# One fixed order for prompt attention and the sample tokens' cached attention

## The chip, the cores and the metric

The kernel runs on one core of a Trainium2 chip. The metric is device time in microseconds (us) of one execution, the median of three runs. The core has five engines with queues of their own: TensorE (PE, matrix products and transposes), VectorE (DVE), ScalarE (ACT), GpSimd (POOL) and SyncE (SP, which issues most transfers). PE writes only into PSUM, eight banks of 128 partitions x 512 floats; DVE and ACT copy from there.

## What is computed

One step of a one-layer decoder, for a prompt of 1024 tokens and for 8 sample tokens at position 4096: a half step of a SwiGLU network (1024 to 2816 features and back), a token mixer, a second half step, with norms before each. The mixer has four GLA heads (a recurrence with gates) and four MLA heads (attention over a compressed latent). The change lies in the mixer. Its two attentions are, in short:

```
# prompt, per head and block of 128 queries
s = (q_nope @ k_nope.T + q_pe @ k_pe.T) * scale      # keys up to the query
o = softmax(s) @ v                                    # k_nope = lat @ w_uk, v = lat @ w_uv
# sample tokens, 4096 cached keys and the token's own, absorbed form
s = (q_lat @ lat_all.T + q_pe @ pe_all.T) * scale     # q_lat = q_nope @ w_uk.T
o = (softmax(s) @ lat_all) @ w_uv
y = concat([y_gla, y_mla]) @ w_out
```

The cached latents lie in pages, and a page table says where.

## The kernel before, in words

Every large product is made from fp32 operands split in a high and a low part (`split`, L84 to L86: ACT writes the high part, DVE the difference), and `mm3` (L88 to L95) adds three passes: high x high, high x low, low x high.

A tile framework builds the program. Each tile comes from a pool with a number of buffers for its tag; a new tile waits until an old one of its tag has been read for the last time, and a pool that is opened where another was closed waits for that one's tiles. A planner at build time sets the order of each engine's instructions by the place in the text, earlier first, with what is ready; `tc.high_priority` moves some ahead. At run time each engine runs its queue in that order.

The stages that matter here, in the order of the text: the GLA of the prompt, in `levels` and `chunks(0)` to `chunks(3)` (L990 to L1025, two chunks of 128 tokens each, each needing the state that the one before left); between them `gate(0)` to `gate(3)` (L1071 to L1078), each 72 matmuls over the mixer's input; `gate_out` writes the gated outputs to DRAM (`ygs`). Before, `gate(3)` stands after `chunks(3)`.

Then comes the attention of the sample tokens. It is cut in 16 units, two groups of four tokens times eight stretches of 512 keys. `dec_unit` (L1157) fetches four latent tiles `kvt` and four rotary tiles `pet` with eight indirect transfers that POOL issues (L908), turns them with PE transposes against an identity into the bank `pd` (L1168, L1176; 24 transposes, copied out as `peT` by DVE and `latT` by ACT), makes the scores (L1181, L1184), the softmax (L1154, L1155), turns the probabilities (L1190) and multiplies them with the latents (L1195). `dec_combine` adds the token's own key and joins the eight parts. Two units are made before the prompt's attention (`decode(2)`), then one after each of its sixteen steps.

A step of the prompt's attention is a head h (four) and a block m of 256 queries (four). `scores(m)` projects the queries, makes for both blocks of 128 queries up to two score tiles `sc` (L1355 to L1361), takes the maximum on DVE (L1363), the exponentials on ACT (L1370) and scales them on DVE (L1376). `outputs` of the step before then turns the probabilities (L1391, m + 1 groups of four transposes), splits them (`pT_h`, `pT_l`) and multiplies with the values into `po`. For each pair of heads the rotary queries are made first (`rope`, L789 to L800), then the values; for each head the keys.

After the attention the GLA outputs come back (`yraw`, L1432 to L1437; POOL's small copy from `ym_h` holds the load back) and are split to `yg_h`, `yg_l`, and `project` (L1445) multiplies with `w_out`. `raw` is a tag with four buffers of 4 KB.

Of the kernel before, what the change touches and what calls it, by code (L numbers as in the profile page):

```python
# [10 lines left out]
F32 = mybir.dt.float32  # L11
# [30 lines left out]
def host_constants():  # L42
    """Tables that follow from the shapes alone."""
# [25 lines left out]
def hybrid_step(ctx: ExitStack, tc: tile.TileContext, I, O, C):  # L69
# [44 lines left out]
    # ------------------------------------------------------------------ norm statistics  # L114
# [7 lines left out]
    def sumsq(acc, sqp, src, m, n, eng=None):  # L122
        """acc[:, :n] (+)= src^2 for feature tile m."""
# [7 lines left out]
    def token_rstd(r, acc, sqp, L, inv_n):  # L131
        """r[:, i] = 1/sqrt(mean + eps) of the i-th 128 of L tokens, from the per-partition partial sums acc."""
# [10 lines left out]
    def spread_all(R, r, sqp, L, scale=1.0):  # L143
        """R[:, token] = scale * r on every partition, for L tokens."""
# [8 lines left out]
    def rstd(R, acc, sqp, s, inv_n, scale=1.0):  # L153
        """R = scale / sqrt(mean + eps) of block s on every partition."""
# [5 lines left out]
    def spread(r, sqp, ps, n, scale=1.0):  # L160
        """ps = scale * r, one value per token on its partition, on every partition."""
# [62 lines left out]
    def left_blocks(w, p, plain=False):  # L224
        """For the outputs 2p and 2p + 1 (of 128 features each) of w."""
# [56 lines left out]
    def eight(A, B, n, evict, between=None):  # L282
        """The plain products: evict(o, C[o // 2][o % 2])."""
# [9 lines left out]
    def first_steps(wg, wu, B, k0, loaded, between=None):  # L293
        """The first k0 pairs of outputs for the first tokens, from plain products."""
# [12 lines left out]
    # The down product is cut in the same way, with the even and the odd tiles of hidden features as the halves of features in.  # L307
    # Its right-hand blocks, in the order t1, t2, t3, t4, B11, B21, B22; two tiles of features of both chunks at a time.
# [5 lines left out]
    def sums_out(c, p, b, t):  # L314
        """Right-hand blocks of the hidden features 2p and 2p + 1, b = B11, B12, B21, B22; t is scratch."""
# [9 lines left out]
    def gate_up(wg, wu, B, k0, start, loaded):  # L325
        """silu(wg x) * (wu x) in hd; the first k0 pairs of outputs are made for the second tokens only, at the end."""
# [19 lines left out]
    def quarter(Q, pl, wd, name, order):  # L346
        """Name aij: the half j of the features in (even or odd tiles) to the half i of the features out."""
# [101 lines left out]
    # ================================================================== load x, first half step  # L449
# [15 lines left out]
    def token_factor(i, c):  # L465
        """1 / rms of 128 tokens, one on each partition: for the first tokens on a diagonal, for the others times x in place."""
# [23 lines left out]
    def natural(c, q, ts):  # L490
        """The normalized input of the tokens CH[c], with features on partitions, as the halves q; the 128 tokens ts."""
# [38 lines left out]
    def new_xT():  # L530
        """x of all tokens, with features on partitions: x(c, m, h)."""
# [61 lines left out]
    def residual1(i):  # L593
        """Adds 128 tokens' x."""
# [16 lines left out]
    def split1(c, m, h):  # L611
        """The mixer's input, from x(c, m, h)."""
# [1047 lines left out]
```

## Time and profile before

| what | value |
|---|---|
| median of three runs | 2168.03 us (2167.33 to 2170.8) |
| the profiled execution: span from first to last instruction | 2100.6 us |
| PE busy in it | 2030.7 us (97%) |
| DVE, ACT, POOL busy | 1487.7, 842.9, 191.8 us |
| mean granted clock of PE | 0.988 |
| PE's chain at the end of the page: lines L94 and L410 | 35% of the span |

The profile is of one execution; its own time is known only as its span. Times in the tables below are us from the span's start. A matmul's duration is the time from its start to its modelled end, and the next one starts long before that, so the distance of two starts says what one costs, and a busy PE isn't one that works at its peak. PEclk is the granted clock as a share of the full 2.4 GHz; it has two levels here, 1.0 and 0.5. The attention of both kinds of tokens lies from about 1020 to 1306 us.

### The profile page before, as it was taken

Reading aid. Unit: us, or ns where it says so; the run is one execution under the profiler, and the core shown is the slowest. Engines: PE = TensorE matmul, PEld = TensorE weight load, DVE = VectorE, ACT = ScalarE, POOL = GpSimd, SP = SyncE. Lnnn points to the kernel's source line nnn. Section 1 sums busy time; section 2 is a strip of 40 time slices with the busy share of each in tenths; the row PEclk is TensorE's granted clock in tenths of the full one; section 3 lists DMA queues with packets and bytes.
Section 4 is the critical chain, followed back from the end, with each engine's and each line's share of the span. In section 5 each row is a group of like instructions: output and inputs, shape, how many; then the busy total and the mean of one; then the engine's idle time right before and its main releaser. Section 6 shows DMA issues by size and latency. Waiting matters only on the chain. (4 is left out here: it accounts for less than half of the span.)

```text
span 2100.6 us, 40499 instructions
## 1 busy us (share of the span) xinstructions
PE 2030.7 (97%) x16354; PEld 1917.7 (91%) x16354; DVE 1487.7 (71%) x2917; ACT 842.9 (40%) x1563; POOL 191.8 (9%) x223
## 2 busy tenths in 40 slices
PE   7999999999999999899799998999999999999997
PEld 7999999999999988788567676899999999999997
DVE  7877777794877774865566666488777777766775
ACT  6432322343445431445554554244322322333534
POOL 1000000000000001311454350000000000000000
PEclk9999999999999999999899998999999999999999
DMA  6233223357254422012433242643223223474352
GB/s 211 73 102 116 86 92 116 97 191 273 93 174 130 115 54 76 21 41 61 143 116 115 94 144 73 191 152 108 95 89 119 89 92 117 158 260 146 109 158 92
DMA packets 205292, 251.13 MB, mean 120 GB/s; under 512 B 23336, under 2 KB 165840, under 8 KB 205104
## 3 DMA queue, kind: packets, MB, share of 16 engines
q1 hardware_dynamic: 196912, 223.36, 33.8%
q0 software_dynamic: 8192, 25.17, 3.8%
q8 instruction: 129, 2.11, 0.4%
q14 instruction: 59, 0.48, 0.1%
HBM read 189.18 MB, written 59.30 MB: 118 GB/s over the span
## 5 line engine op out<-in xcount | busy, mean ns | idle before, releaser
L94 PE MATMUL pp<-bh,ah 128*128 128x260 f32 (+1 forms) x2432 | 687.2, 283 | 3.0 <-ACT bh L85 2.5
L94 PE MATMUL pp<-bl,ah 128*128 128x260 f32 (+1 forms) x2432 | 688.1, 283 | 1.2 <-DVE bl L86 1.2
L94 PE MATMUL pp<-bh,al 128*128 128x260 f32 (+1 forms) x2432 | 688.8, 283 | 0.2 <-DVE al L86 0.2
L94 PEld LDWEIGHTS pp<-bh,ah 128*128 128x128 f32 x2432 | 459.3, 189 | 3.3 <-ACT bh L85 2.7
L94 PEld LDWEIGHTS pp<-bl,ah 128*128 128x128 f32 x2432 | 458.5, 189 | 1.9 <-DVE bl L86 1.9
L94 PEld LDWEIGHTS pp<-bh,al 128*128 128x128 f32 x2432 | 458.8, 189 | 0.4 <-DVE al L86 0.4
L410 PE MATMUL pp<-tl,dh 128*128 128x256 f32 x1232 | 248.7, 283 | 0.1
L410 PE MATMUL pp<-th,dh 128*128 128x256 f32 (+1 forms) x1232 | 248.5, 283 | 0.0
L410 PE MATMUL pp<-th,dl 128*128 128x256 f32 x1232 | 248.4, 282 | 0.1
L85 ACT ACTIVATE ah<-raw 128x512 fp32r<-128x512 f32 x208 | 129.0, 628 | 257.7 <-PE pp L94 243.9
L410 PEld LDWEIGHTS pp<-tl,dh 128*128 128x128 f32 x1232 | 189.9, 188 | 2.4 <-DVE tl L86 2.4
L410 PEld LDWEIGHTS pp<-th,dh 128*128 128x128 f32 x1232 | 190.7, 189 | 0.1
L410 PEld LDWEIGHTS pp<-th,dl 128*128 128x128 f32 x1232 | 189.7, 188 | 0.3 <-DVE dl L86 0.3
L86 DVE TENSOR_TENSOR al<-raw,ah 128x512 fp32r<-128x512 f32 x208 | 142.8, 691 | 61.7 <-ACT ah L85 61.5
L85 ACT ACTIVATE dh<-a 128x1024 fp32r<-128x1024 f32 (+1 forms) x84 | 83.0, 988 | 248.7 <-PE pp L410 224.8
L86 DVE TENSOR_TENSOR dl<-a,dh 128x1024 fp32r<-128x1024 f32 (+1 forms) x84 | 95.3, 1135 | 115.9 <-ACT dh L85 109.5
L85 ACT ACTIVATE ah<-sl 128x512 fp32r<-128x512 f32 x132 | 83.1, 631 | 213.9 <-PE pp L94 166.8
L94 PE MATMUL pw<-xh,wh 128*128 128x260 f32 (+4 forms) x320 | 100.9, 315 | 0.0
L94 PE MATMUL pw<-xl,wh 128*128 128x260 f32 (+4 forms) x320 | 99.8, 312 | 0.0
L94 PE MATMUL pw<-xh,wl 128*128 128x260 f32 (+4 forms) x320 | 99.5, 311 | 0.0
L86 DVE TENSOR_TENSOR tl<-traw,th 128x1032 fp32r<-128x1032 f32 (+1 forms) x84 | 95.7, 1139 | 3.0 <-ACT th L85 2.7
L86 DVE TENSOR_TENSOR al<-sl,ah 128x512 fp32r<-128x512 f32 x132 | 90.6, 688 | 8.1 <-ACT ah L85 4.3
(426 smaller groups left out, 3698.9 us busy)
## 6 DMA issues: line engine op xcount, KB each, us to landing
traw<-td SPq DMA_DIRECT2D x70, 516.0 KB, 3.5
raw<-in_ffn_w_gate_dram SPq DMA_DIRECT2D x52, 512.0 KB, 4.5
raw<-in_ffn_w_up_dram SPq DMA_DIRECT2D x52, 512.0 KB, 4.0
a<-in_ffn_w_down_dram SPq DMA_DIRECT2D x40, 512.0 KB, 7.5
td<-q SPq DMA_DIRECT2D x22, 520.0 KB, 4.6
td<-q SPq DMA_DIRECT2D x22, 512.0 KB, 3.7
raw<-in_w_out_dram SPq DMA_DIRECT2D x16, 512.0 KB, 4.7
td<-q SPq DMA_DIRECT2D x22, 260.0 KB, 4.1
```

Source lines behind the costliest of these rows:

```text
L85: S.activation(out_h, src, AF.Copy)
L86: eng.tensor_sub(out_l, src, out_h)
L94: PE.matmul(ps, w_, x_, start=i == 0, stop=i == n - 1)
L410: PE.matmul(bank[c][m], w_[:, kk, ms], x_[:, kk, c * N[0]:c * N[0] + N[c]], start=first and j == 0 and (c == 1 or m % 2 == 0), stop=last a ...
```

## The change

The units of the sample tokens lose `dec_unit`. Its parts become functions of their own: `fetch`, `turn` (one of six groups of four transposes and the copy out), `dec_scores`, `dec_softmax`, `dec_turn`, `dec_values`, and `dec_combine` is cut into `dec_own` and `dec_combine`, generators whose pieces `tick` runs two at a time. Of the two PSUM banks of the units one ("pt") now serves all turns, and the other ("sc") one unit's scores, then its turned probabilities, then its output. Two early units are still made before, with the planner's order. The rest is a loop over the sixteen steps that writes out the place of each piece; the keys of the unit after next are fetched, and those of the next unit turned, while a unit is worked on. At the end, each instruction of PE, ACT and DVE made since the start of the loop's preparation is tied to the one before it in the text.

Some work changes place: the probabilities are scaled on ACT; small weights and the rope tables are loaded through the tag `raw`; `w_uv` for the sample tokens is loaded at the end, through `raw` too; `kvt` has 11 buffers and `pet` 8, where both had 6; the values are made two blocks a step. `gate(2)` and `gate(3)` go ahead of `chunks(2)`. `project` takes the GLA part (`yg`) before the MLA part (`ym`).

```diff
...
-    psD_cm, psd = pool("psD", 2, space=PSUM, side="right")
+    psD_cm, psd = pool("psD", 1, space=PSUM, side="right")
+    def dbank(tag="pt"):
+        return psd.tile([P, 512], F32, name=tag, tag=tag)
...
+    def turn(g, u, i):
+        kvt, pet = got[g, u]
+        p = dbank()
+        for q in range(4):
...
+            PE.transpose(p[:, q * P:(q + 1) * P], src, ident)
...
+        if i < 4:
+            S.activation(t_, p, AF.Copy)
+        else:
+            V.tensor_copy(t_, p)
...
-    gate(2)
     chunks(1)
+    gate(2)
+    gate(3)
     chunks(2)
     chunks(3)
-    gate(3)
...
+    load_uqr(0); rotary(0, 0); load_uk(0); keys(0, 0); load_uv(0)
+    values(0, 0); values(0, 1); rotary(0, 1); load_uq(0); queries(0, 0)
+    for i in range(6):
+        turn(*units[0], i)
+    for i, (h, m) in enumerate(steps):
...
+        if third:
+            fetch(*third)
+        s0 = scores(h, m, 0)
+        d(dec_scores)
+        maximum(*s0)
+        if m == 3 and h < 3:
+            load_uk(h + 1)
...
+        pr0 = exps(*s0, 0)
+        d(dec_softmax)
+        t(0)
+        s1 = scores(h, m, 1)
+        maximum(*s1)
+        factor(*s0)
+        tick()
+        if old:
+            old.turn(0); old.part(0); old.turn(1); old.part(1)
+        d(dec_turn)
+        pr1 = exps(*s1, 1)
+        t(4)
+        if m == 3 and h == 1:
+            rotary(1, 0)
+        t(1)
+        if old:
+            old.product(0); old.turn(2); old.part(2)
+        scale(pr0, s0[1])
+        factor(*s1)
+        tick()
+        if i and h % 2 == 0:
+            values(h // 2, 2 * m)
+        t(5)
+        if old:
+            old.product(1); old.turn(3); old.part(3)
...
+        d(dec_values)
+        tick()
+        scale(pr1, s1[1])
+        t(2)
...
+        if m == 1:
+            keys(h, 1)
+        if m == 3 and h < 3:
+            keys(h + 1, 0)
+            if h == 1:
+                rotary(1, 1); load_uq(2)
+        if old:
+            old.product(2)
+        t(3)
+        tick()
+        if new:
+            queries(*new)
+        if old:
+            old.product(3); old.out()
...
+    uv = rawp.tile([P, 4, P], F32, name="uvr", tag="raw")
+    ld.dma_start(uv, w_uv)
     for h in range(4):
         p = dbank()
         PE.matmul(p[:, :NS], uv[:, h], oT[:, :, h], start=True, stop=True)
         split(ym_h[:, h, SEQ:], ym_l[:, h, SEQ:], p[:, :NS])
+    for ins in list(traced[first:]):
+        if ins.engine in (PE, Activation, DVE):
+            if ins.engine in last:
+                tc.add_manual_dep(ins, last[ins.engine].name, NoSync)
+            last[ins.engine] = ins
...
-                mm3(p, [ym ... for k in range(4)] + [yg ... for k in range(4)])
+                mm3(p, [yg ... for k in range(4)] + [ym ... for k in range(4)])
```

Some lines are joined or shortened here. `t(k)` is `turn` of the next unit, `d` runs a piece of the present unit, `old` is the step before: `turn(j)`, `part(j)` and `product(j)` are the transposes, the split and the six passes of its j-th pair of key blocks, for j up to its m, and `out` the split into `ym`.

## Rows read from the trace of the kernel before

**Rows 1.** The head of the page.

```profile
span 2100.6 us, 40499 instructions
```

**Rows 2.** Busy time of each engine in four stretches. The columns: stretch and its length, then PE, PE's weight loads, DVE, ACT and POOL with busy us and number of instructions, the granted clock, the share of the DMA engines, GB/s.

```profile
980.70:1018.30 37.60, 33.48 (x202) 26.59 (x200) 21.23 (x56) 22.16 (x85) 5.88 (x5) 1.00 0.09 31
1018.30:1065.60 47.30, 32.08 (x245) 21.95 (x244) 28.20 (x57) 27.07 (x53) 32.08 (x31) 0.82 0.58 183
1065.60:1283.00 217.40, 211.31 (x1903) 159.50 (x1904) 133.19 (x324) 109.54 (x264) 94.57 (x102) 1.00 0.35 108
1283.00:1306.30 23.30, 19.87 (x116) 16.77 (x115) 19.62 (x52) 13.24 (x32) 0.00 (x0) 0.85 0.17 46
```

**Rows 3.** PE's timeline inside the steps: start, us, engine, line, operation, out<-in, shape, count; instructions of one kind are merged.

```profile
1102.52 0.40 PE L1359 MATMUL sc<-kp_l,qs 128*128 128x512 f32 x1
1102.76 0.40 PE L1355 MATMUL sc<-k_h,q_h 128*128 128x512 f32 x1
...
1103.98 1.04 PE L1391 MATMUL ps<-ident,pp 128*128 128x128 f32 x8
...
1105.22 0.28 PE L94 MATMUL po<-pT_h,v_h 128*128 128x256 f32 x1
1105.34 0.28 PE L94 MATMUL po<-pT_l,v_h 128*128 128x256 f32 x1
...
1119.07 1.08 PE L1195 MATMUL pd<-kvt,dpT 128*32 128x128 f32 x32
...
1128.37 1.20 PE L1181 MATMUL dsc<-latT,qlp 128*32 128x512 f32 x7
...
1129.47 1.39 PE L1184 MATMUL dsc<-peT,qpp 128*32 128x256 f32 x13
```

**Rows 4.** Groups of ACT and DVE instructions from 1020 to 1310 us: line, engine, operation, out<-in, shape, count | busy us, mean ns of one | idle time before it.

```profile
L1178 ACT ACTIVATE latT<-pd 128x512 f32<-128x512 f32 x64 | 37.7, 598 | 26.1 <-PE pd L1176 24.7
L85 ACT ACTIVATE pT_h<-ps 128x512 fp32r<-128x512 f32 x40 | 23.1, 597 | 32.1 <-PE ps L1391 30.5 <-PE po L94 1.5
L85 ACT ACTIVATE q_h<-ps 128x256 fp32r<-128x256 f32 x16 | 6.1, 380 | 14.2 <-PE ps L94 14.2
L1301 ACT ACTIVATE qs<-qpr 64x512 fp32r<-64x512 f32 x8 | 5.0, 624 | 0.3 <-DVE qpr L800 0.2
L796 ACT ACTIVATE sw<-ps 32x512 f32<-32x512 f32 x8 | 4.7, 589 | 1.6 <-PE ps L94 1.4
...
L86 DVE TENSOR_TENSOR pT_l<-ps,pT_h 128x512 fp32r<-128x512 f32 x40 | 27.0, 689 | 7.8 <-ACT pT_h L85 7.4
L1171 DVE COPY peT<-pd 128x512 f32<-128x512 f32 x32 | 21.5, 684 | 9.5 <-PE pd L1168 9.5
L86 DVE TENSOR_TENSOR q_l<-ps,q_h 128x256 fp32r<-128x256 f32 x16 | 6.8, 422 | 3.8 <-ACT q_h L85 3.8
L1302 DVE TENSOR_TENSOR qs<-qpr,qs 64x512 fp32r<-64x512 f32 x8 | 5.5, 687 | 1.6 <-ACT qs L1301 1.4
L800 DVE TENSOR_TENSOR qpr<-qpr,sw 128x512 f32<-128x512 f32 x4 | 2.7, 684 | 0.0
```

**Rows 5.** One hand-off from PE to ACT to DVE, in the timelines of the three engines.

```profile
1287.14 0.49 PE L1391 MATMUL ps<-ident,pp 128*128 128x128 f32 x3
...
1287.72 0.60 ACT L85 ACTIVATE pT_h<-ps 128x512 fp32r<-128x512 f32 x1 [2.03 <-PE ps L1391]
...
1288.36 0.69 DVE L86 TENSOR_TENSOR pT_l<-ps,pT_h 128x512 fp32r<-128x512 f32 x1 [0.44 <-ACT pT_h L85]
```

**Rows 6.** The entry: the first two key fetches on POOL and the first load of rotary query weights on SP, from their timelines, the first rotary matmul on PE, and the score matmuls of one line (duration min/median/max, first and last start).

```profile
1019.98 1.18 POOL L908 DMA_INDIRECT kvt<-in_cache_kv_dram,idx  x1 [0.19 <-DVE G L1083]
...
1024.34 0.95 POOL L908 DMA_INDIRECT pet<-in_cache_pe_dram,idx  x1 [0.30 <-issue]
...
1029.91 0.93 SPq L1281 DMA_DIRECT2D uqr<-in_mla_w_uq_dram  x2
...
1039.70 0.50 PE L94 MATMUL ps<-qn_h,uqh 128*128 128x512 f32 x1
...
L1355 PE MATMUL sc<-k_h,q_h x48: 278/391/501, 1065.6 to 1292.2; 128*128 128x512 f32 x24, 128*128 128x256 f32 x16, 128*128 128x384 f32 x8
```

**Rows 7.** Two idle times of PE, in brackets with what ended them, and the busy time by stretch around or after each, with the columns of rows 2.

```profile
850.02 2.30 PE L949 MATMUL pg<-qt,E 128*128 128x128 f32 x11 [1.83 <-DVE qt L945]
...
850.80:854.20 3.40, 3.40 (x17) 3.14 (x16) 2.19 (x5) 0.00 (x0) 0.11 (x1) 0.50 0.00 0
...
932.38 0.33 PE L984 MATMUL ps<-ident,on 128*128 128x128 f32 x1 [1.63 <-ACT on L981]
...
929.00:937.00 8.00, 6.37 (x35) 4.96 (x34) 4.01 (x11) 4.96 (x24) 3.33 (x4) 1.00 0.12 37
```

**Rows 8.** The exit: the split of `yraw` on ACT, the last product and the first matmul of the projection on PE, SP's longest wait (us in total, times, longest), and the page's row of the `w_out` loads (KB each, median us from issue to landing).

```profile
1296.45 2.01 ACT L85 ACTIVATE yg_h<-yraw 128x1024 fp32r<-128x1024 f32 x2
...
1306.05 0.28 PE L94 MATMUL po<-pT_h,v_l 128*128 128x256 f32 x1
1309.12 0.77 PE L94 MATMUL pr<-ym_h,wh 128*128 128x512 f32 x1 [2.79 <-issue]
...
SPq L1439 <- DVE yg_l L86: 38.2, 1, 38.2
...
raw<-in_w_out_dram SPq DMA_DIRECT2D x16, 512.0 KB, 4.7
```

More of the change, by code (lines that the diff above doesn't have):

```diff
@@ L1182, in dec_unit @@
+            grp[g] = [ep.tile([P, 3, NU + 1], F32, name="stat", tag="stat"), None]
+        sc = dbank("sc")
+        live[g, u] = [sc]
+        for bi in range(4):
+            PE.matmul(sc[rows[bi], :], qlp[:, 4 * g + bi], turned.pop((g, u, bi)), start=True, stop=False)
+        pe = [turned.pop((g, u, 4 + b2)) for b2 in range(2)]
         for par in range(2):
             for bi in range(4):
[L1184 removed]
@@ L1213, in dec_combine @@
         V.tensor_copy(pnT, p[:NS, :P])
+        yield
         p = dbank()
@@ L1237, in hybrid_step @@
     units = [(g, u) for g in range(2) for u in range(NU)]
-    def decode(n):
-        for g, u in units[:n]:
-            dec_unit(g, u)
-            if u == NU - 1:
-                dec_combine(g)
-        del units[:n]
-    decode(2)
+    EARLY = 2
+    fetch(*units[0])
+    fetch(*units[1])
+    for n in range(EARLY):
+        fetch(*units[n + 2])
+        for i in range(6):
+            turn(*units[n], i)
+        for f in (dec_scores, dec_softmax, dec_turn, dec_values):
+            f(*units[n])
+    units = units[EARLY:]
     close(gw_cm)
@@ L1406, in hybrid_step, with tick @@
-    outputs(*pend)
+    traced = tc.nc.cur_bb.bb.instructions
+    first = len(traced)
+    W, UK, UV, Qm = {}, {}, {}, {}
+    qs_ = [ap_.tile([P, SEQ], F32R, name=f"qs{hh}", bufs=1) for hh in range(2)]
+    v_h, v_l = [ap_.tile([P, 8, 256], F32R, name=f"v_{z}", bufs=1) for z in "hl"]
+    k_h, k_l = [ap_.tile([P, SEQ], F32R, name=f"k_{z}", bufs=1) for z in "hl"]
+    slack = []
+    def tick():
+        for _ in range(2):
+            if slack and next(slack[0], slack) is slack:
+                slack.pop(0)
@@ new lines, in values, with keys, queries @@
+    def values(t, j):
+        js, (uv_h, uv_l) = slice(j * P, (j + 1) * P), UV[t]
+        p = bank()[:, :256]
+        for i, (l_, r_) in enumerate(((lat_h, uv_h), (lat_l, uv_h), (lat_h, uv_l))):
+            PE.matmul(p, l_[:, js], r_, start=i == 0, stop=i == 2)
+        split(v_h[:, j], v_l[:, j], p)
+    def keys(h, b):
+        s = slice(b * 512, b * 512 + 512)
+        p = bank()
+        mm3(p, [(*UK[h], lat_h[:, s], lat_l[:, s])])
+        split(k_h[:, s], k_l[:, s], p)
+    def queries(h, m):
+        p = bank()[:, :256]
+        wt, s = W[h], QB[m]
+        mm3(p, [(wt[0][:, k], wt[1][:, k], qn_h[:, k, s], qn_l[:, k, s]) for k in range(2)])
+        Qm[h, m] = [ap_.tile([P, 256], F32R, name=f"q_{z}", tag=f"q_{z}") for z in "hl"]
+        split(*Qm[h, m], p)
@@ new lines, in hybrid_step, with d, t @@
+    load_uqr(0)
+    rotary(0, 0)
+    load_uk(0)
+    keys(0, 0)
+    load_uv(0)
+    values(0, 0)
+    values(0, 1)
+    rotary(0, 1)
+    load_uq(0)
+    queries(0, 0)
+    for i in range(6):
+        turn(*units[0], i)
+    steps = [(h, m) for h in range(4) for m in range(4)]
+    old = None
+    for i, (h, m) in enumerate(steps):
+        unit, after, third = [units[j] if j < len(units) else None for j in range(i, i + 3)]
+        new = steps[i + 1] if i + 1 < len(steps) else None
+        def d(f, *a):
+            if unit:
+                f(*unit, *a)
+        def t(k):
+            if after:
+                turn(*after, k)
+        if third:
[6 more added lines that the diff above has]
+            if h == 1:
+                load_uqr(1)
+                load_uv(1)
+            else:
+                load_uq(h + 1)
+        pr0 = exps(*s0, 0)
[6 more added lines that the diff above has]
+        if old:
+            old.turn(0)
+            old.part(0)
+            old.turn(1)
+            old.part(1)
+        d(dec_turn)
[5 more added lines that the diff above has]
+        if old:
+            old.product(0)
+            old.turn(2)
+            old.part(2)
+        scale(pr0, s0[1])
[5 more added lines that the diff above has]
+        if old:
+            old.product(1)
+            old.turn(3)
+            old.part(3)
+        if unit and unit[1] == 0:
+            while slack:
+                tick()
[3 more added lines that the diff above has]
+        t(2)
+        if i and h % 2 == 0:
+            values(h // 2, 2 * m + 1)
+        if m == 1:
+            keys(h, 1)
+        if m == 3 and h < 3:
+            keys(h + 1, 0)
+            if h == 1:
+                rotary(1, 1)
+                load_uq(2)
+        if old:
+            old.product(2)
+        t(3)
+        tick()
+        if new:
+            queries(*new)
+        if old:
+            old.product(3)
+            old.out()
+        old = Values(h, m, (pr0, pr1))
+        if unit:
+            g, u = unit
+            if u == NU - 4:
+                slack.append(dec_own(g))
+            if u == NU - 1:
+                while slack:
+                    tick()
+                slack.append(dec_combine(g))
@@ L1407, in hybrid_step @@
+    old.turn(0)
+    old.turn(1)
+    old.part(0)
+    old.part(1)
+    tick()
+    for j in range(4):
+        old.product(j)
+        old.turn(j + 2)
+        tick()
+        old.part(j + 2)
+        tick()
+    old.out()
+    while slack:
+        tick()
+    uv = rawp.tile([P, 4, P], F32, name="uvr", tag="raw")
+    ld.dma_start(uv, w_uv)
     for h in range(4):
@@ L1410, in hybrid_step @@
         split(ym_h[:, h, SEQ:], ym_l[:, h, SEQ:], p[:, :NS])
+    last = {}
+    for ins in list(traced[first:]):
+        if ins.engine in (mybir.EngineType.PE, mybir.EngineType.Activation, mybir.EngineType.DVE):
+            if ins.engine in last:
+                tc.add_manual_dep(ins, last[ins.engine].name, mybir.DependencyInfo(
+                    mybir.DependencyClass.NoSync, mybir.DependencyReason.DATA), reason="in the order of the text")
+            last[ins.engine] = ins
     close(a_cm)
```

327 lines of the change are left out of this document (154 added, 173 removed).

## The prediction, made before the change was run

> **What bounds the kernel now.** I read the page first (the span [rows 1], busy shares, clock), then the busy time by stretch [rows 2], then TensorE's timeline inside the stretch that the change rewrites, then the durations on ScalarE and VectorE there, and last the queue of loads. TensorE (PE) is the engine of the whole kernel, and the change touches only 980 to 1315 us of it. Three parts are to be seen in [rows 2]. From 1018.3 to 1065.6 PE is busy 32.1 of 47.3 us at a mean clock of 0.82: the entry, where it waits for cached keys. From 1065.6 to 1283.0 it is busy 211.3 of 217.4 us: the sixteen steps of prompt attention with fourteen units of the sample tokens between them. From 1283.0 to 1306.3 it is busy 19.9 of 23.3 us at 0.85: the last steps, with nothing left to put between.
>
> Busy is not useful. From pitches [rows 3]: a 512-column pass starts every 0.23 us, a 256-column pass every 0.12, a transpose every 0.11 (eight in 1.04, the last one's 0.27 taken off), a unit's score matmuls take 2.2 (1128.37 to 1130.86, less 0.28), its value matmuls 0.8. Per head there are scores of 4864 columns in five passes (11.1), ten transpose groups of 0.44, ten products of six passes (7.2), four query projections (2.9) and the keys (1.4): 27, times four is 108. Add values 5, the second rotary pair 3, fourteen units at 2.2 + 0.44 + 0.8 (48) and the transposes of thirteen units (6 x 0.44 each, 34): 198 us of work in the 240.7 us from 1065.6 to 1306.3. The excess is 43: 6 of idle before 1283, some 27 lost at alternations of kinds of matmul, the rest in the tail.
>
> **The change, part by part.** No matmul goes away; the order is what changes, and PE, ScalarE (ACT) and VectorE (DVE) now each run in the order of the text.
>
> *The six turns of a unit.* Each `turn` fills the one "pt" bank with four transposes and has it copied out (ACT for 0 to 3, DVE for 4 and 5); the next turn waits for that copy. In the step's text `t(4)` stands directly before `t(1)`. Count from the start X of `old.turn(0)`. PE needs 4 x 0.44 = 1.76 for `old.turn(0)`, `old.turn(1)`, `dec_turn` and `t(4)`. The copies run so: the first group can be read at X + 0.60 (0.49 for three plus one pitch), hand-off 0.09 [rows 5]; ACT makes two high parts of 0.60 [rows 4], to X + 1.89; DVE makes the second low part (0.69), the copy for `dec_turn` (of the shape of peT, 0.68) and that of `t(4)` (0.68): X + 3.98 with the hand-off. `t(1)` stands until then: 2.2 us. Behind it on PE are the first product and all that follows; no other work is free to pass. With one old group (m = 1) it is 1.9; at m = 0 ACT comes later and it is about 2.8. Thirteen steps have turns: 28 us. Bounds: 13 where DVE is far ahead (a bare copy and hand-offs, 1.0 each), 40 where a tick adds DVE work.
>
> *The other turns.* A turn through one bank takes 0.60 + 0.6 to 0.69 + two hand-offs, 1.35. Between `t(1)` and `t(5)` stand 0.44 + 0.72, between `t(5)` and `t(2)` at least 0.44 + 0.8, between `t(2)` and `t(3)` at m = 2 only 0.44. Mean wait 1.0 a step: 13 (bounds 5 and 20).
>
> *Queries at the end of a step.* The next score needs q_h (0.38) and, two passes later, q_l (0.42) [rows 4], with nothing between except at m = 0: 0.75 in twelve steps, 9.
>
> *The second rotary pair,* in one step. Each block is a chain of four ACT copies (0.59), three DVE operations (0.68) and the four that make qs: some 8 us, and the turns and the next query weights stand behind it in both queues: 13 in all (bounds 5, 18).
>
> *First products and the tail:* 5. Alternations: the text groups kinds, so I take 11 in place of 27.
>
> Steps: 198 + 28 + 13 + 9 + 13 + 5 + 11 = 277, against 240.7: **+36**. By the low bounds it is 240, no change; by the high ones 301.
>
> *The entry.* Six chunk passes took 37.6 us before (980.7 to 1018.3 [rows 2]), 6.3 each, gate matmuls in their gaps. With gates 2 and 3 ahead of the last two `chunks`, the gates end near 1000, the cached keys are asked for there and not at 1019.98 [rows 6], and the two early units run in the gaps of the last four passes. These still end near 1025. The weights of the first rotary block were asked for at 1029.91, once GLA's space was free, and its matmul began at 1039.70. I let that matmul begin at 1031. The start before the first score is now a fixed row: rotary 8, keys and values 3, rotary 8, query weights and queries 2, six turns one after another at 1.35 (8), that is 29 to 31. First score at 1061, before it was at 1065.6: **-5**. Bounds: -16 (matmul at 1020), +6 (early units late by as much as before).
>
> *The clock.* After 1.83 us of idle PE fell to half (1.2 GHz) for 850.8 to 854.2; after 1.63 us it stayed at 1.00 [rows 7]. Thirteen stalls of 2 to 3 us lie above both. I take nine falls, each with some 2.4 us of work in 3.4 us of half clock, half of that lost: **+10** (bounds 0, 25). A rule speaks on this: the Trainium skill, "TensorE: Matmul & The Clock Gate", section "A second HAM failure mode: psum-queue depth-cycling", says that a loop which cycles PSUM banks can let PE idle briefly so often that its clock swings between its two levels. By it every pass is followed by a fall, 13 x 1.2 = 16 in place of 10; no row shows it in this loop yet.
>
> *The exit.* Before, the last product was issued at 1306.05 and the projection began at 1309.12 [rows 8]. The four yraw tiles had long been loaded (the small load behind them waited 38.2 us for a low part), but the split began only at 1296.45, when the sample tokens' last matmuls had read oT. Now those matmuls stand behind the last product: four of them, one bank, about 0.6 each (2.4). Then split (ACT 1.05 by the row's two in 2.01; DVE about 1.2), a w_out load into the freed slot (4.7), and its split (2.3): 11 in place of 3.1, **+8**. That the projection now takes yg first helps nothing while yg is what is late. Bounds: 0 (yg's space free earlier), +12 (the fourth yraw, behind uvr's slot).
>
> *At nothing:* scaling the probabilities moves from DVE to ACT, some 29 us on an engine that is busy 109.5 of 217.4 [rows 2], and its place is in the walk above. Key fetches are the same number, two steps ahead, eight a step at 0.95 + 0.30 [rows 6] = 10 us under a step of 17 on GpSimd; without that cover a late key would hold all of PE. The weight loads on SyncE (rope tables, uq, uk, uv) wait for slots of "raw"; they come early, and only uvr keeps its slot to the end (in the exit).
>
> Sum: +36 - 5 + 10 + 8 = **+49**. The profiled execution has only its span, 2100.6; the median of the runs, 2168.03, lies 67.4 above, and I leave that. Span 2150, time **2217 us**.
>
> **Rivals.**
> *Faster.* The fixed order removes most alternations and the idle tail, and copies keep up: steps 198 + 11 + 10 = 219 (-22), entry -16, exit 0: 2130. For it: PE lost 43 us in steps. Against: the 2.2 us at `t(1)` follow from five rows and one bank. It holds if that wait is below 0.5.
> *The order does not bind* or is mostly what the planner chose: steps as before, entry -10, exit 0: 2158.
> *No change.* Low bounds in the steps (0), entry -8, exit +8: 2168.
> *Far slower.* The clock falls after each pass and stays (25 in place of 10), and the sample tokens' own keys and sums, eight more fills of the "pt" bank between turns, cost 1.35 each (11); exit +12: 2217 + 30 = 2247. It decides if the mean clock in the steps is below 0.85.
>
> **How the numbers follow.** Forecast 0.60 (its own range 2188 to 2242), faster 0.13, order not binding 0.05, no change 0.07, far slower 0.15. The range 2155 to 2258 leaves out the fast rival and the end of the slow one. A difference under 0.2%, 4.3 us, cannot be told from none. Faster 0.18, same 0.07, slower 0.75.
>
> **What would show it.** In the changed kernel's waits of PE the copy of peT by DVE stands first, 25 us or more over thirteen times, and waits of `turn` together reach 40. Steps take 14 to 20 us, the one with two rotary blocks over 28. First score near 1061, last product near 1347, projection some 11 later. Half clock shows inside the steps, where before it was 1.00 throughout. Wrong if PE's idle time in the steps is under 30 us, or if the first score comes before 1050.

## The result, and the profile after

The changed kernel takes **2202.45 us** (median of 2198.21 to 2204.1), the kernel before beside it 2169.41: a ratio of 1.0148, interval 1.0131 to 1.0166, so 1.5% slower. The forecast was 2217, range 2155 to 2258, so the time lies inside and the sign is right. How the time comes about isn't what the prediction said, and for a reason that it had in its hands and left lying: the 67.4 us between the span of its trace and the timed runs.

Of the changed kernel, the profiled execution took 2202.13 us at a span of 2200.4, a difference of 1.7. The kernel before, profiled once more, took 2174.89 at a span of 2173.1. So some 1.7 us lie outside the span, not 67, and the trace with 2100.6 was of an execution that was itself 66 us shorter. Later runs show the same gap between chips: the kernel before takes 2178 us on one chip and 2099 to 2101 on two others. By its span the trace of [rows 1] is of the quicker kind of chip, and by their times the runs beside it are of the slower kind. ("Kind" is a name for these two groups. The slower runs with a known chip are all of one chip on one occasion, so the chip and the occasion can't be told apart.) Each kind needs its own comparison:

| us | quicker: before (first trace) | quicker: changed | slower: before (second trace) | slower: changed |
|---|---|---|---|---|
| first score at | 1065.6 | 1082.6 | 1074.4 | 1089.7 |
| first score to last product | 240.5 | 295.0 | 304.7 | 302.8 |
| last product to projection | 3.1 | 13.6 | 3.1 | 13.9 |
| projection to last matmul | 781.1 | 783.0 | 780.5 | 783.6 |
| span | 2100.6 | 2184.5 | 2173.1 | 2200.4 |

On the slower kind, where the result was measured, the change adds 27.3 us of span: 15.3 before the first score, 10.8 + 3.1 behind the last product, and -1.9 in the steps. On the quicker kind it adds 83.9: 17.0 + 54.5 + 10.5 + 1.9. (In time it is 33 on the slower kind: the second trace of the kernel before took 2174.89, the runs beside the changed kernel 2169.41.) The steps cost nothing on the slower kind and most on the quicker, since the kernel before has stalls of its own on the slower kind: PE idles 48.4 us in its steps there and 9.5 on the quicker, the changed kernel 61.6 and 53.7.

The busy time by stretch, with the columns of [rows 2]; in each fence the stretch up to the first rotary matmul (or up to a few us ahead of it), from there to the first score, and the steps. First the changed kernel on the slower kind, with the exit as a fourth line:

```profile
978.00:1048.20 70.20, 56.49 (x346) 42.06 (x344) 33.34 (x79) 36.89 (x108) 30.99 (x30) 0.93 0.35 108
1048.20:1089.70 41.50, 23.70 (x116) 14.25 (x116) 13.77 (x26) 13.15 (x25) 12.38 (x13) 0.60 0.31 95
1089.70:1392.60 302.90, 241.34 (x2031) 186.79 (x2030) 141.72 (x344) 144.06 (x341) 88.09 (x95) 0.92 0.23 72
1392.60:1406.40 13.80, 1.92 (x10) 1.54 (x8) 5.82 (x10) 6.25 (x11) 0.17 (x1) 0.57 0.81 223
```

The changed kernel on the quicker kind:

```profile
978.00:1043.20 65.20, 52.19 (x320) 38.75 (x320) 30.59 (x73) 32.91 (x94) 29.71 (x29) 0.92 0.36 112
1043.20:1082.60 39.40, 23.18 (x115) 13.85 (x116) 13.63 (x25) 13.15 (x25) 12.52 (x14) 0.65 0.34 104
1082.60:1377.70 295.10, 241.37 (x2031) 187.80 (x2030) 141.87 (x344) 144.62 (x341) 88.15 (x95) 0.91 0.24 74
```

The kernel before on the slower kind:

```profile
981.00:1038.20 57.20, 42.85 (x240) 30.88 (x238) 31.25 (x76) 30.69 (x97) 22.67 (x22) 0.85 0.36 113
1038.20:1074.40 36.20, 24.35 (x192) 17.66 (x191) 17.64 (x34) 17.79 (x37) 16.46 (x17) 0.91 0.34 106
1074.40:1379.20 304.80, 256.34 (x2017) 187.37 (x2017) 152.99 (x375) 122.79 (x295) 93.12 (x100) 0.89 0.26 79
```

Read the third number from the end of a line, the granted clock: in [rows 2] the steps ran at 1.00 (up to 1283); here they run at 0.91 to 0.92 in the changed kernel and at 0.89 in the kernel before on the slower kind. And read PE's busy time against the stretch: some 54 to 62 us idle in the changed kernel's steps on either kind.

What PE waited for in the steps of the changed kernel (the view of waits: engine, line waited at, releaser: us in total, times, longest), quicker kind:

```profile
PE pt L1157 <- DVE peT L1162: 22.8, 12, 2.6
PE pt L1157 <- ACT latT L1160: 7.3, 6, 4.5
PE sc L1386 <- ACT q_h L85: 5.7, 12, 0.5
PE ps L94 <- ACT uqh L85: 5.2, 1, 5.2
PE pt L1250 <- DVE om L1247: 3.9, 2, 3.3
PE pt L1227 <- DVE pnT L1224: 3.4, 2, 1.7
```

The first line is the prediction's main step: `t(1)` standing behind VectorE's copy of peT. One such place, in the timelines of PE, ScalarE and VectorE:

```profile
1177.63 0.60 PE L1157 MATMUL pt<-ident,pet 128*128 128x128 f32 x4
1180.02 0.66 PE L1157 MATMUL pt<-ident,kvt 128*128 128x128 f32 x4 [1.79 <-DVE peT L1162]
...
1177.45 0.60 ACT L85 ACTIVATE pT_h<-ps 128x512 fp32r<-128x512 f32 x1 [0.29 <-PE ps L1437]
...
1178.08 0.69 DVE L86 TENSOR_TENSOR pT_l<-ps,pT_h 128x512 fp32r<-128x512 f32 x1 [0.37 <-ACT pT_h L85]
1178.69 0.68 DVE L1194 COPY dpT<-sc 128x512 f32<-128x512 f32 x1
1179.29 0.68 DVE L1162 COPY peT<-pt 128x512 f32<-128x512 f32 x1
```

PE had filled the bank by 1178.2, and VectorE came to it only after the low part and the copy for `dec_turn`.

### The profile page after: what moved, and what is told of

It is laid out like the page before. It is cut to its first block, busy times and chain, and to the rows that moved or that the text cites. A ratio compares the mean times of both kernels' runs of the same rounds, so it can differ in the third digit from the quotient of the medians.

```text
span 2200.4 us, 40492 instructions
## 1 busy us (share of the span) xinstructions
PE 2057.1 (93%) x16354; PEld 1937.6 (88%) x16354; DVE 1478.4 (67%) x2885; ACT 867.5 (39%) x1611; POOL 190.7 (9%) x223
## 4 chain that ended last, share of the span: by engine, by line
PE 85%; DVE 6%; ACT 4%; issue 2%; POOL 1%; DMA 1%; SPq 0%; another core or an unknown queue 0%; POOLq 0%; ACTq 0%; DVEq 0%
PE pp L94 41%; PE pp L410 19%; PE pw L94 5%; PE pr L94 4%; PE pt L1157 2%; PE ps L94 1%; PE po L1454 1%; PE pw L1039 1%; PE pg L937 1%; PE sc L1176 1%; DVE pT_l L86 1%; PE sc L1204 1%; PE sc L1181 1%; DVE qt L933 1%; ACT latT L1160 1%
```

## The experiments

Each time stands beside the kernel before on the same chip, since the two kinds differ by more than any edit. "Fixed order" means the ties between instructions of PE, ScalarE and VectorE.

**The kernel before once more** (slower kind), with a trace of its own. No edit.

> The kernel before, unchanged, with a trace of its own, since its timed runs (2168) lie 67 us above the span of the trace that the prediction read (2100.6), while the changed kernel's runs lie 1.7 to 1.8 us above their spans. Theory A (the traced execution was quicker than the timed ones): the span of this one is time less 1.8, near 2166, and the 66 us sit in one or two stretches, not spread. Then the change's +33 in time is far less than the +100 between the two traces. Theory B (the 67 us lie outside any span): span near 2100, time near 2168.

2175.87 against 2178.38, ratio 0.9991 (0.998 to 1.0001); span 2173.1 at 2174.89. Theory A. The two traces are of the same program and agree within 2.4 us up to 1043 and within 0.6 us in the length of what follows the projection's begin; the difference lies between, in the stretch in which the cached keys are fetched.

**One turn moved** (slower kind):

```diff
-        t(4)
+        t(1)
         if m == 3 and h == 1:
             rotary(1, 0)
-        t(1)
         if old:
             old.product(0)
+        t(4)
+        if old:
...
```

> The changed kernel with t(1) in the place of t(4) and t(4) in the place behind the first product. Theory A (the prediction's step: PE stands at t(1) for VectorE's copy of peT, 24.1 us over 14 waits in the changed kernel's trace): these waits fall under 8 us in total and the time falls by 10 to 24 us, to 2178 to 2192. Theory B (with one bank the wait only passes to the next turn, t(5), which now follows t(4) closely): PE's waits of turns together stay near 42 us and the time stays within 5 us of 2202.

2213.65 against 2178.38, ratio 1.0174 (1.0145 to 1.0202). Theory B by the waits; the ratio's interval overlaps with the changed kernel's (1.0131 to 1.0166), so worse isn't shown. In the steps the waits for peT fall from 23.4 to 10.5 us, but the turns also wait 14.1 for latT and 9.9 with no releaser that the profile shows, 34.5 together against 37.1; they no longer gather at one place (24 waits of up to 5.7 us, where the changed kernel has 21 of up to 4.5). The view of waits of this kernel's steps:

```profile
PE pt L1157 <- ACT latT L1160: 14.1, 11, 4.9
PE pt L1157 <- DVE peT L1162: 10.5, 10, 5.7
PE pt L1157 <- issue: 9.9, 3, 4.8
```

So it isn't that pair of turns that costs; six turns through one bank in a fixed order cost in either place that was tried.

**No fixed order** (slower kind). The loop over `traced[first:]` is taken out; nothing else.

> The changed kernel without the ties that put PE, ScalarE and VectorE in the order of the text; everything else as changed. Theory A (the fixed order costs, since nothing may pass a waiting turn): the steps shorten by 25 us or more, 2177 or less. Theory B (the one bank and the planner's costs hold the order anyway): within 8 us of 2202. Theory C (the ties hold back a worse order): slower than 2210.

2140.87 against 2178.38, ratio **0.9835** (0.9815 to 0.9854): its span is 61.5 us below the changed kernel's, by the two ratios it is nearer 70, and it is faster than both on this kind of chip. Theory A by more than it asked. First score at 1070.1 (1089.7 with the fixed order), steps 272.2 (302.8), last product to projection 3.3 (13.9).

**The gates where they stood** (slower kind; fixed order kept):

```diff
+    gate(2)
     chunks(1)
-    gate(2)
-    gate(3)
     chunks(2)
     chunks(3)
+    gate(3)
```

> The changed kernel with the gates where they stood: gate(2) ahead of chunks(1), gate(3) behind chunks(3). In the changed kernel's trace the last chunks have no gate matmuls beside them (1003 to 1041 at a low clock), and the first score comes at 1089.7. Theory A (the gates' move lengthens the entry): the first score comes 10 to 20 us sooner, time 2182 to 2192. Theory B (the gates' matmuls cost the same wherever they stand, and the cached keys are what is late): within 5 us of 2202. Theory C (prediction: the earlier key fetches are worth it): slower by 5 to 12 us.

2205.76 against 2178.38, ratio 1.0117 (1.0087 to 1.0147), which overlaps with the changed kernel's 1.0131 to 1.0166: theory B. The first rotary matmul comes at 1037.5 in place of 1048.2, and the first score at 1094.8 in place of 1089.7: what the gates gain ahead of the attention, the fixed order gives back, and more, before the first score. The 10.7 us of the first rotary matmul count below, at the entry.

**Fixed order in the steps alone** (quicker kind). `first` is set at the loop over the steps, and the ties end ahead of the load of uvr:

```diff
+    first = len(traced)
     steps = [(h, m) for h in range(4) for m in range(4)]
...
+    ends = len(traced)
     uv = rawp.tile([P, 4, P], F32, name="uvr", tag="raw")
...
-    for ins in list(traced[first:]):
+    for ins in list(traced[first:ends]):
```

> The changed kernel with the fixed order only from the first step to the last product: what prepares the steps (rotary queries, keys, values, six turns) and the sample tokens' last four matmuls with what follows are left to the planner. In the changed kernel the first rotary matmul to the first score takes 41.4 us and the last product to the projection 13.9; without any fixed order 24.7 and 3.3. Theory A (entry and exit are half of what the fixed order costs): these two fall to about 25 and 3, the steps stay near 303, time 2172 to 2180. Theory B (the steps hold the cost, and what is saved at the entry comes back as a wait for the next unit): within 8 us of 2202.

2157.04 against 2098.61, ratio 1.0278 (1.0261 to 1.0295). The expectation was made for the slower kind; against the changed kernel on the quicker kind (2187.35, below) it is 30.3 less, theory A in the two stretches, though 30 of the 83 us that the fixed order costs on this kind are a third and not half. From the first rotary matmul to the first score it takes 17.6 us (39.4), from the last product to the projection 3.2 (13.6); the steps stay at 296.7.

**More buffers in the kernel before** (quicker kind):

```diff
...
-name="kvt", tag="kvt", bufs=6
+name="kvt", tag="kvt", bufs=8
-name="pet", tag="pet", bufs=6
+name="pet", tag="pet", bufs=8
...
```

> The kernel before with eight buffers in place of six for the cached latents and for the rotary keys (room for them from one buffer in place of two for dpp and dpT and a narrower oT). In the second trace of the kernel before PE waits at turns of latents whose transfer was issued 4.9 to 5.3 us earlier, once the unit before had freed its buffers. Theory A (late keys are what makes a usual execution 66 us longer than the one in the first trace): steps fall from 305 toward 245 us, time 2110 to 2140. Theory B (the clock or the order of the planner makes the difference, and keys are no more than a part): 2155 to 2175.

2100.03 against 2098.61, ratio 1.0 (0.9991 to 1.001). On this kind the kernel before has no late keys to begin with, so the run says that the buffers cost nothing and can gain nothing here; it can't tell its theories apart for the slower kind, and that wasn't tried there.

**No fixed order, six buffers** (quicker kind). `kvt` and `pet` go from 11 and 8 back to 6 in the kernel without the fixed order.

> The changed kernel without the fixed order and with the six buffers of the kernel before for cached latents and rotary keys. Theory A (the earlier fetches are what makes the version without the fixed order 37 us faster than before): back to 2165 to 2185. Theory B (the order of the planner, given the new text, does it): 2140 to 2150.

2139.78 against 2098.61, ratio 1.0196 (1.0179 to 1.0213). The numbers of the expectation were for the slower kind. Beside the same kernel with 11 and 8 buffers on this kind (2104.35, below) the six cost 35.4 us, as theory A has it for the buffers; that they make the gain of the slower kind wasn't measured there. PE waits for the transfers themselves (waits in the steps):

```profile
PE pt L1157 <- DMA kvt<-in_cache_kv_dram,idx: 17.8, 17, 2.8
```

The kernel before lives with six, since a unit's turns come just ahead of its own scores. The new text turns the next unit while the present one still holds its latents for `dec_values`, and for that six are too few. The waits are not all of it: the steps take 280.2 us in place of 244.3, of which 15 are idle time and some 5 the clock; the remaining 16 us are not explained.

**No fixed order, gates where they stood** (quicker kind). Both edits from above.

> The changed kernel without the fixed order and with the gates where they stood. With the fixed order this move brought the first rotary matmul 10.7 us sooner (1048.2 to 1037.5) and gave it all back before the first score. Theory A (without the fixed order the gain stays): 2128 to 2136. Theory B (the early units and keys take it back): within 4 us of 2141.

2103.14 against 2098.61, ratio 1.0025 (1.0015 to 1.0035). Against 2104.35 with the gates moved: 1.2 us apart, with intervals that overlap, so without the fixed order the gates' place is worth nothing in time. It does move the entry: the first rotary matmul comes at 1038.40 in place of 1046.91 and the first score 6.1 us sooner, and the stretches behind the first score give most of it back (2.3 us each in the steps and in the projection).

**The changed kernel on the quicker kind.** No edit.

> The changed kernel, unchanged, beside the kernel before on one chip. Two chips have now shown the kernel before at 2178 (first four runs) and at 2099 (next four); the trace that the prediction read is of the second kind (span 2100.6), the timed runs of before and of the changed kernel beside it of the first. Theory A (the change adds the same everywhere): 30 to 35 us above the kernel before on either kind of chip. Theory B (on the quicker kind the kernel before has no stalls to give back, so all that the fixed order costs shows): on a chip where before takes 2099, 2175 to 2195, 75 to 95 above; on a chip where it takes 2170 to 2180, 2198 to 2206 as recorded.

2187.35 against 2101.03, ratio **1.0418** (1.0401 to 1.0436): 86 us above, theory B.

**Two banks for the turns** (quicker kind; fixed order kept):

```diff
-    psB_cm, psc = pool("psB", 3, space=PSUM)
+    psB_cm, psc = pool("psB", 2, space=PSUM)
+    psP_cm, psp = pool("psP", 1, space=PSUM)
+    second.append(psp)
...
-        p = dbank()
+        p = second[0].tile([P, 512], F32, name="pt", tag="pt") if second and i > 2 else dbank()
```

> The changed kernel, fixed order and all, with two PSUM banks in place of one for the turns in the steps (t(0), t(1), t(2) in one, t(3), t(4), t(5) in the other, so that they alternate); the second is taken from the score tiles, which have two in place of three. Theory A (the one bank is what makes PE wait at the turns, 42 us in the steps): these waits fall below 12 us, the score tiles' lack of a bank gives back 5 to 15, and the time is 12 to 30 us below the changed kernel on the same chip. Theory B (the order binds at other places as much, or the lost score bank costs the same): within 8 us of the changed kernel on the same chip. Theory C: slower by more.

2157.56 against 2101.03, ratio 1.0274 (1.0257 to 1.0292): 29.8 us below the changed kernel, theory A at its upper end. The steps fall from 295.0 to 267.2 us. The turns' waits, 30.1 us above, are the first and the last of these (waits of the steps):

```profile
PE pt L1159 <- DVE peT L1164: 3.2, 6, 0.9
PE sc L1390 <- ACT pp L1411: 3.0, 2, 1.7
...
PE pt L1159 <- ACT latT L1162: 2.7, 1, 2.7
```

The score bank that was given up shows as 3.0 us in the line between. Against the kernel without the fixed order (2104.35, next) 53 us are left: 19.5 before the first score, 22.9 in the steps, 9.9 at the exit.

**No fixed order, again** (quicker kind).

> The changed kernel without the fixed order, as once before; on the slower kind of chip it took 2140.9, 37 us below the kernel before. On the quicker kind two neighbours of it are known: with six buffers 2139.8, with the gates where they stood 2103.1. If the job falls on the quicker kind: theory A (the gates' place is most of the 37 us between these two): 2130 to 2140. Theory B (the buffers are most of it, since with six PE waits 17.8 us for latents): 2103 to 2115. If it falls on the slower kind, it is a repeat: 2137 to 2145.

2104.35 against 2100.92, ratio 1.0019 (1.0009 to 1.0029). Theory B: the buffers are most of the 37 us. The busy time from the first rotary matmul to the first score, and of the steps:

```profile
1046.90:1064.50 17.60, 15.03 (x107) 8.26 (x107) 9.38 (x20) 10.51 (x22) 11.29 (x11) 1.00 0.68 212
1064.50:1308.90 244.40, 238.43 (x2045) 179.30 (x2045) 146.99 (x357) 152.10 (x354) 89.60 (x97) 1.00 0.30 93
```

PE is idle 6 us in the steps and its clock is full throughout, at the same instructions that take 295.0 us in the fixed order.

**The same, with the gates where they stood and ym first** (quicker kind).

> The changed kernel without the fixed order, with the gates where they stood and with the projection taking ym first as before: what is left of the change is the text of the steps, the buffers, the scaling on ScalarE and the loads. Theory A (this part of the change is worth having where transfers and hand-offs are late, and nothing elsewhere): on the quicker kind of chip within 5 us of the kernel before (2099), on the slower kind 30 to 55 us below it (2123 to 2148). Theory B (the projection's order is worth 2 us or more by itself: 783.0 against 781.1 from the projection's begin): on the quicker kind at or below the kernel before.

2103.45 against 2100.92, ratio 1.0014 (1.0004 to 1.0024). Within 5 us, as theory A has it; the projection's order is worth nothing (783.2 us from its begin to the last matmul, 783.0 with yg first). The half of theory A that concerns the slower kind wasn't measured for this version.

The ledger of the quicker kind, in times: before 2099 to 2101; the change without its fixed order 2104; with the order in the steps 2157; with the order at the entry and the exit too 2187. On the slower kind: before 2178, without the order 2141, with it 2202. No version beats the kernel before on the quicker kind; on the slower one the change without the fixed order beats both.

## Why the prediction was right, and where it was not

*The time.* 2217 came from 67.4 us left as they were and 49 added. On the quicker kind, from which every row came, the change adds 86, on the slower one, where it was timed, 33. The forecast lies between the two by luck: **the failing step is the first one, "the profiled execution has only its span, 2100.6; the median of the runs, 2168.03, lies 67.4 above, and I leave that".** Where both are known of one execution, time and span differ by 1.7 to 1.8 us. A gap of 3% says that the trace isn't of such a run, and then its idle times and clock needn't be those of the runs either.

*The steps,* taken on the quicker kind, where the rows hold. Predicted with the clock 287 us, measured 295.0. By parts, from the changed kernel's trace: the distances of matmul starts less the pitches of [rows 3] (201.1 in all) and less the idle time (53.7) leave 40.2, of which 16.7 falls where the clock was full (alternations) and 23.5 where it was half. Predicted were 198, 68, 11 and 10. So the waits were there and a fifth smaller, and the clock cost more than twice as much. What the order was to save, it did save: without the ties the same text takes 244.3 us at full clock with 5.9 idle, so some 37 go to alternations, against 17 in the fixed order. The order buys 20 us there and pays 48 in idle time and 23 in clock.

One sum of the prediction is wrong: its low bounds in the steps add up to 246 (198 + 13 + 5 + 9 + 5 + 5 + 11), not 240, so that the rival of no change had 5 us less room than it says.

*`t(1)` behind peT.* 22.8 us in twelve steps, 1.9 each, where 28 in thirteen was forecast at 2.2; at the place shown, with one old group, 1.79 where 1.9 was worked out (its own terms give 2.06 there). The forecast added whole durations of VectorE; in the rows above its three operations begin 0.60 to 0.61 apart though each lasts 0.68 or 0.69, which takes some 0.15 off. That the one bank under a fixed order is the cause, two banks show (-29.8); without the fixed order the one bank alone costs nothing of the kind. That this pair of turns is the culprit, as the prediction made it look, is refuted: with the pair pulled apart nothing was gained.

*The other turns* took 2.8 (13 forecast), *the second rotary pair* 9.7 (13): one wait of 4.5 for latT and one of 5.2 for the query weights. *The queries* took 5.7 in twelve steps (9). The sample tokens' own keys and sums, which the slow rival priced at 11, took 7.3 (om 3.9, pnT 3.4).

*The entry* was the step that failed by most: -5 forecast, +17.0 measured (quicker kind), +15.3 (slower). Of the 22 us between, 12 lie ahead of the first rotary matmul and 9 between it and the first score. It was to begin at 1031 and began at 1043.2. The gates end where the prediction said (at 997, "near 1000"), and the last product of the chunks' state ends at 1026.9 ("near 1025"). But the last transposes of the chunks' normalized outputs end at 1035.4, where they ended at 1022.6 before; the 1018.3 from which the prediction took 6.3 us a pass is the end of the last gate matmul. The rows (PE in the kernel before and in the changed one, then SP, VectorE and ScalarE of the changed one, quicker kind):

```profile
1021.75 0.86 PE L984 MATMUL ps<-ident,on 128*128 128x128 f32 x2 [0.80 <-ACT on L981]
...
1034.67 0.75 PE L972 MATMUL ps<-ident,on 128*128 128x128 f32 x2
...
1036.82 0.90 SPq L1301 DMA_DIRECT2D uqr<-in_mla_w_uq_dram  x2
...
1035.55 1.22 DVE L86 TENSOR_TENSOR qn_l<-raw,qn_h 128x1024 fp32r<-128x1024 f32 x1
...
1042.64 0.42 ACT L85 ACTIVATE uqh<-uqr 128x256 fp32r<-128x256 f32 x1 [0.58 <-DMA ropew<-const_cos_dram]
```

The rotary weights were asked for at 1036.82 and not at 1029.91 as in [rows 6]. They now go through `raw`, whose slots are held by qn, lat and kp until these have been split; the second of these four splits ends, on VectorE, at 1036.77. The prediction put the loads through `raw` at nothing ("they come early"). The slots hand the lateness on, but they don't make it: with the gates where they stood, the same load through the same slots is asked for at 1022.69, ahead of the kernel before (SP and PE, gates where they stood, planner's order, quicker kind):

```profile
1022.69 0.38 SPq L1301 DMA_DIRECT2D uqr<-in_mla_w_uq_dram  x1
...
1038.40 0.50 PE L94 MATMUL ps<-qn_h,uqh 128*128 128x512 f32 x1
```

With the gates moved that load stands at 1039.87 and the matmul at 1046.91 in the planner's order; in the fixed order, on the slower kind, moving the gates back brings the matmul from 1048.2 to 1037.5. So the late begin comes with the move of the gates, which the prediction had down as a gain.

From the first rotary matmul to the first score it took 39.4 us, not 29 to 31: PE's own row of chains was right, but the mean clock was 0.65, so that each of the six turns one after another took 1.8 in place of 1.35. One wait is 6.3, for the query weights, whose split stands in ScalarE's fixed order behind the whole second rotary block (PE's timeline):

```profile
1070.98 0.58 PE L94 MATMUL ps<-qn_h,uqh 128*128 128x256 f32 x1 [6.34 <-ACT uqh L85]
...
1074.55 1.12 PE L1157 MATMUL pt<-ident,kvt 128*128 128x128 f32 x4 [0.69 <-ACT latT L1160]
1076.35 1.11 PE L1157 MATMUL pt<-ident,kvt 128*128 128x128 f32 x4 [0.69 <-ACT latT L1160]
```

That the fixed order makes this, is shown: with the order in the steps alone it is 17.6.

A queue that the prediction named but didn't price: the earlier key fetches stand on GpSimd ahead of the small power of the GLA's norm, and the chunks wait for it (ScalarE, quicker kind). The last four of these powers began at 998.59, 1005.90, 1012.69 and 1018.74 before and begin at 1005.62, 1018.27, 1025.83 and 1031.85 now: 7 us later at first, 13 at the end, most of the growth in the pass with the longer of the two waits below. The fetches go ahead of the chunks only since the gates do, and no run tells the share of this queue from that of the gates' place:

```profile
1006.70 0.37 ACT L969 ACTIVATE on<-ps,gss 128x128 f32<-128x128 f32 x1 [3.53 <-POOL gss L964]
...
1019.35 0.37 ACT L969 ACTIVATE on<-ps,gss 128x128 f32<-128x128 f32 x1 [5.59 <-POOL gss L964]
```

*The exit.* +8 forecast, +10.5 and +10.8 measured. The chain is the one that was drawn, at the end that the bound of +12 named, the fourth yraw (SP, ScalarE and PE, quicker kind):

```profile
1380.79 0.59 PE L1583 MATMUL pt<-oT,uvr 128*128 128x8 f32 x2 [0.47 <-DVE ym_l L86]
1391.20 0.79 PE L94 MATMUL pr<-yg_h,wh 128*128 128x512 f32 x1 [9.81 <-ACT wh L85]
...
1381.71 0.33 SPq L1617 DMA_DIRECT2D yraw<-ygs  x1
...
1386.65 1.06 ACT L85 ACTIVATE yg_h<-yraw 128x1024 fp32r<-128x1024 f32 x1 [1.90 <-DMA yraw<-ygs]
...
1390.09 1.06 ACT L85 ACTIVATE wh<-raw 128x1024 fp32r<-128x1024 f32 x1 [2.20 <-DMA raw<-in_w_out_dram]
```

The four small matmuls of the sample tokens end the fixed order; behind them come yraw, its split, the loads of `w_out`, their split. Without the ties the 13.6 are 3.3.

*The clock.* Nine falls were forecast and nine began in the steps (quicker kind), but the half clock lasts 54.3 us together (3.1 of it from a fall that began before the first score), not 31, and it cost 23.5. Four of the nine last 3.4 us, as in [rows 7], four 6.8 and one 10.2. Nor is a fall decided by how long the stall just before it was: of the twelve waits for peT five were followed by one at once; a wait of 1.98 us at 1303 was and one of 1.98 at 1144 was not. The Trainium skill, "TensorE: Matmul & The Clock Gate", section "A second HAM failure mode: psum-queue depth-cycling", says that a loop which cycles PSUM banks can make the clock swing by its brief idle times. The trace agrees in so far as the clock swings where PE idles at a bank: in the fixed order the steps run at 0.91, in the planner's order, at the same matmuls and with the same single bank for the turns, at 1.00. But there were nine falls in sixteen steps, not one behind each pass, and three of the nine stand at other waits (two in the second rotary pair, one at om).

*The rivals.* "Faster" asked for a wait below 0.5 at `t(1)`; it was 1.9. "The order does not bind" is refuted by the 83 us between the kernel with and without it on the quicker kind. "Far slower" did not get its condition: the mean clock in the steps was 0.91 to 0.92, above its 0.85, though the exit and the projection behind it came to its +12 (10.5 + 1.9, quicker kind). Of the signs that were named, peT did stand first, with 22.8 us for the 25 asked, but the waits of `turn` came to 30 and not 40, and the last product to 1377.6 and not 1347.

## What to carry to other kernels

Before a sum is made, hold the trace's span against the timed runs beside it: if they differ by per cents, the trace is of another kind of execution, and its waits and its clock belong to that one alone. An order written out for several in-order engines makes each bank and each copy in it a place where everything behind stands; here the same text under the planner's order cost 0.2% on one kind of chip and gained 1.6% on another, so tie only what a measurement has shown to go wrong without. Work that fills the gaps of a chain costs little where it stands: with the gates moved ahead and the key fetches behind them, the last chunk ended 12.8 us later, and the weights, the splits and the first rotary matmul followed it. Ask what ends last after the move, not only what starts sooner.

## What the runs showed of the hardware that was not expected

The same program takes 2099 to 2101 us on two chips and 2178 on a third, and the difference lies between about 1040 us and the last product. There, on the slower kind, ScalarE and VectorE begin late behind PE at some places. In the first trace no copy of a turned latent for which ScalarE had stood idle begins more than 0.46 us after the turn's last matmul was issued (30 of them); in the second it is up to 4.22 us (46). One such place, VectorE's maximum of a unit's scores; in the kernel before on the quicker kind:

```profile
1039.81 0.69 DVE L1154 TENSOR_REDUCE stat<-dsc 128x1 f32<-128x512 f32 x1 [1.88 <-PE dsc L1184]
```

and on the slower kind:

```profile
1041.14 0.69 DVE L1154 TENSOR_REDUCE stat<-dsc 128x1 f32<-128x512 f32 x1 [4.54 <-PE ps L94]
```

PE's next matmul behind these scores is issued at 1039.70 on the quicker chip [rows 6] and here:

```profile
1038.23 0.50 PE L94 MATMUL ps<-qn_h,uqh 128*128 128x512 f32 x1
```

so that the maximum follows it by 0.1 us there and by 2.9 here. In the steps PE is idle 48.4 us in place of 9.5, and the other 25 of the 64 us go with the clock, at half for 68 us in place of 7. What it costs depends on the kernel: before loses 77 us to it, the change without the fixed order 37, and the changed kernel 15, perhaps because its engines already stand waiting elsewhere. Slower transfers don't show: the packets of the cached keys' queue took 3.8% of the 16 DMA engines' time in the first trace and 3.7% of the longer second one, some 80 us in both. The traces of the slower kind hold no landing times, so a wait for a transfer may stand there under another name or none. Why the two kinds differ stays open; no run was made that could tell.
